# Tokens' low parts behind the next weight tile, list steps in a second queue, last transposes behind the product

## The chip, the cores and the metric

The kernel runs on one core of one Trainium2 chip. The metric is the device time of one execution in microseconds. Before the change the median of three runs is 1836.94 us (1836.01 to 1843.89). The engines are TensorE (PE), VectorE (DVE), ScalarE (ACT), GpSimd (POOL) and SyncE (SP, which here only issues DMAs).

## What is computed

Two blocks work on 512 tokens of width 1024 in float32. The first is an mLSTM and pooling mixer followed by a mixture of 32 experts; the second is a stick-breaking attention beside a gated spatial mixing. The change touches the experts alone. Cut to what matters:

```python
logits = xt @ w_router + b_router
top_vals, top_idx = lax.top_k(logits, 4)          # each token goes to 4 of 32 experts
top_gates = jax.nn.softmax(top_vals, axis=-1)
...
def expert_block(xb, e):                          # the rows of expert e
    gate = jnp.minimum(xb @ w_gate[e] + b_gate[e], 7.0)
    up = jnp.clip(xb @ w_up[e] + b_up[e], -7.0, 7.0)
    glu = gate * jax.nn.sigmoid(1.702 * gate)
    return (glu * (up + 1.0)) @ w_down[e] + b_down[e]
# each result times its gate, added to its token's row
```

Products are made in split precision: a float32 operand becomes a high part (a rounded cast) and a low part (the operand less its high part), and a product is the sum of high x high, high x low and low x high. What is split late or not at all is multiplied raw, at a slower rate.

## The kernel before

The experts are sorted by their number of tokens. A *wide* one has 112 rows (`C`), a *narrow* one 64 (`CS`); experts 0 and 1 and then every odd one to 29 are wide, the even ones from 2 to 28 and 30 and 31 are narrow. For a narrow one the high and low parts of the tokens lie side by side in one stationary operand (`xs`, `as`), so that two matmuls do what three do for a wide one.

`place(s)` is one step of the loop over experts: the gate product of expert s, the transposes of the previous expert's activated rows u into `aT`, the up product of s, the transposes of the next expert's tokens `xg` into `xT`, the gather of the tokens of s + 2, and the down product of s - 1 with its result and scatter. Each product (`product`, L921) goes through four weight tiles of 256 rows by 1024. SP loads the tiles (`wr`, 1 MB each) eight ahead, ACT makes the high part (`wh`, L145), DVE the low part (`wl`, L148), and `LEAD` = 3 tiles are split ahead of the product that uses them. The last tile of the products that have a raw part is not split: it is multiplied with `raws` at full float32.

Inside `manual_schedule` the order of the code is the order on each engine. The list `todo` holds small steps; `product` takes one after each weight tile. Among them are the activation of a narrow gate (`sg`), the clip and the product of u, and `lists`: at experts 1, 4, 8, 12, 16, 20 and 24 it puts four `marks` (L800, DVE) and one `rest` (L806 and following: 16 small matmuls `pl` and six small DVE operations) into `todo`. They make the row lists of four experts.

`parts_T` transposes and splits. A wide operand takes two PSUM tiles, of four transposes each: the first holds 4 of 8 blocks (128x448 when written as 112 columns each), the second 2 blocks that are split (128x224) and 2 raw ones. A narrow one takes one. `hilo` (L183) writes the high part on ACT and then the low part on DVE, which reads the PSUM tile as well as the high part. All of `tp`, `pl`, `pg` and the like come from `bank` (L108), which has two buffers:

```python
return self.ps.tile(list(shape), F32, name=name, tag="B", bufs=2)
```

The products' sums come from another pool (three buffers of two banks). After expert 8 stands a loop for lists that are longer than their expert's rows (`longer_lists`); with these inputs it makes no round. `gates_T`, `places` and `bias` prepare the last results; `before_last` and what follows it finish experts 30 and 31.

Of the kernel before, what the change touches and what calls it, by code (L numbers as in the profile page):

```python
# [25 lines left out]

WIDE = [True, True] + [False, True] * 14 + [False, False]
# [13 lines left out]
def f32(ap):  # L41
    return ap.bitcast(F32)
# [746 lines left out]
    return placed  # L789


def lists(k, places, entries, name, kinds, out, soon):


    nc, n, shp = k.nc, places.shape[2], [P, NTC, P]
    oh4 = k.b4("loh" if n == 1 else "oh4", (P, n, NTC, P), BF)

    def marks(e):
        slots = k.slots[:, kinds[e], None, :].to_broadcast(shp)
        nc.vector.tensor_tensor(oh4[:, e], slots, places[:, :, e, None].to_broadcast(shp), op=OP.is_equal)  # L800

    def rest():
        pt = k.bank("pl")
        for e in range(n):
            for c in range(NTC):
                nc.tensor.matmul(pt[:, 8 * e:8 * e + 5], oh4[:, e, c], entries[:, c, e], start=(c == 0), stop=(c == NTC - 1))  # L806
        L = pt[:, :8 * n].rearrange("p (e w) -> p e w", w=8)
        tok = k.small("tok" + name, [P, n], bufs=2)
        nc.vector.tensor_reduce(tok, L[:, :, :2], axis=X, op=OP.add)
        ti, tf, ga = (k.small(t + name, [P, n], dt, bufs=3) for t, dt in (("ti", I32), ("tf", F32), ("ga", F32)))  # L810
        for kind in sorted(set(kinds)):
            for odd in range(2):
                es = [e for e in range(odd, n, 2) if kinds[e] == kind]
                if es:
                    assert es == list(range(es[0], es[-1] + 1, 2))
                    es = slice(es[0], es[-1] + 1, 2)
                    rows_of(k, tok[:, es], ti[:, es], tf[:, es], kind)
        nc.vector.tensor_reduce(ga, L[:, :, 2:5], axis=X, op=OP.add)
        out.extend((ti[:, e:e + 1], ga[:, e:e + 1], tf[:, e:e + 1]) for e in range(n))

    for e in range(n):
        soon(lambda e=e: marks(e))
    soon(rest)


# [23 lines left out]
def moe(k):  # L849
    nc, tc, a = k.nc, k.tc, k.a  # L850
# [6 lines left out]

    info = []

    def listed(n, soon):  # L860

        s0 = max(2, listed.n)
        listed.n = s0 + n
        ss = slice(s0, s0 + n)
        lists(k, k.posm_s[:, :, ss], k.entry_s[:, :, ss], "l%d" % n, [int(not WIDE[s]) for s in range(s0, s0 + n)], info, soon)

    listed.n = 0
    ti, tf, placed = first_rows(k)
# [3 lines left out]
    k.depth = 9  # L872
    bias_g, bias_u = k.bias

    def raw_part(name, parity):

        return k.fixed["xr"][:, :2] if k.fixed else k.raws[:, 4 * "xa".index(name) + 2 * parity:][:, :2]

    def parts_T(src, name, parity, wide=True):


        if wide:
            hi, lo, raw = *(k.b4(name + n, (P, KD - 2, C), F32R) for n in "hl"), raw_part(name, parity)
            def use(k0, pt):
                n = min(4, KD - 2 - k0)
                k.ondve = k.hilo(pt[:, :n], hi[:, k0:k0 + n], lo[:, k0:k0 + n])
                if n < 4:
                    nc.scalar.copy(raw, pt[:, n:])  # L888

            k.transposes(src[:C], use)  # L890
            return hi, lo, raw
        x, pt = k.b4(name + "s", (P, KD, P), F32R), k.bank("tp", (P, KD, CS))
        for kk in range(KD):
            nc.tensor.transpose(pt[:, kk], src[:CS, kk * P:(kk + 1) * P], k.ident[:CS, :CS])  # L894
        if name == "x":
            k.hilo(pt, x[:, :, :CS], x[:, :, CS:])
            return x,
        k.hilo(pt[:, :KD - 2], x[:, :KD - 2, :CS], x[:, :KD - 2, CS:])
        raw = raw_part(name, parity)[:, :, :CS]
        nc.scalar.copy(raw, pt[:, KD - 2:])  # L900
        return x, raw

    def one_of(s):
        if s < 2:
# [7 lines left out]
    todo = []  # L912

    def product(xT, b, one, get):

        wide, raw = len(xT) == 3, xT[-1] if len(xT) > 1 else None
        p, n = k.bank2("pe"), C if wide else P
        for i in range(2 if b is not None else 0):
            nc.tensor.matmul(p[:n, i], one, b[:, i * 512:(i + 1) * 512], start=True, stop=False, skip_group_check=True)  # L919
        last = KD - 3 if raw is not None else KD - 1  # L920
        for k0 in range(0, KD, 2):  # L921
            w = get()
            for i in range(2):
                kk = k0 + i
                if len(w) == 1:
                    lr = (raw[:, i], w[0]),
                elif wide:
                    lr = (xT[0][:, kk], w[0]), (xT[0][:, kk], w[1]), (xT[1][:, kk], w[0])
                else:
                    lr = (xT[0][:, kk], w[0]), (xT[0][:, kk], w[1])  # L930
                for n_, (l, r) in enumerate(lr):
                    for j in range(2):
                        o = i * D + j * 512
                        nc.tensor.matmul(p[:l.shape[1], j], l, r[:, o:o + 512], start=(b is None and kk == 0 and n_ == 0),  # L934
                                         stop=(kk in (last, KD - 1) and n_ == len(lr) - 1), skip_group_check=True)
            if todo and not k.fixed:
                todo.pop(0)()
        return p[:n].rearrange("p a b -> p (a b)")

    lim = 7.0 / (1.0 + math.exp(-1.702 * 7.0))  # L940

    def soon(f):

        f() if k.fixed else todo.append(f)

    def added(p, name):

# [28 lines left out]
    def down(aT, get):  # L976
        return product(aT, None, None, get)
# [84 lines left out]
    listed(2, lambda f: f())  # L1062
    gather(xgs[0], info[2][0], C if WIDE[2] else CS)

    def place(s, u, xT, one):

        if s == 1 or s % 4 == 0 and s + 4 < NE:
            listed(4, todo.append)
        sg = gate(xT, one, k.next_w)
        aT = parts_T(u, "a", (s - 1) % 2, WIDE[s - 1])  # L1070
        u = up(sg, xT, one, k.next_w)
        if s + 1 < NE:
            one = one_of(s + 1)
            xT = parts_T(xgs[(s + 1) % 2], "x", (s + 1) % 2, WIDE[s + 1])
        if s < NE - 2:
            gather(xgs[s % 2], info[s + 2][0], C if WIDE[s + 2] else CS)
        if s < NE - 1:
            result(down(aT, k.next_w), *info[s - 1][:2])
        if s == NE - 3:
            todo.extend((lambda: places(k, [info[e][2] for e in (NE - 2, NE - 1)]), lambda: gates_T(k),  # L1080
                         lambda: bias(k, "b_down", 0.0, 3)))
        return u, xT, aT, one

    k.lead, k.depth, one = LEAD, DM, one_of(1)
    with tc.manual_schedule(engines=ALL_ENGINES):
        for s in range(1, LOOP_AT + 1):
            u, xT, aT, one = place(s, u, xT, one)
        while todo:
            todo.pop(0)()
    longer_lists()  # L1090
    with tc.manual_schedule(engines=ALL_ENGINES):
        for s in range(LOOP_AT + 1, NE):
            if s == NE - 2:
                k.stop = k.experts_end
            u, xT, aT, one = place(s, u, xT, one)
        aT1 = []
        todo.append(lambda: aT1.append(parts_T(u, "a", (NE - 1) % 2, WIDE[NE - 1])))
        k.depth = DE
        p = down(aT, k.next_w)
    k.lead = 0  # L1100
    with tc.manual_schedule(engines=IN_ORDER):
        before_last(k)
        k.depth = DE2
        k.ready += [k.parts() for _ in range(4 - len(k.ready))]
        ys = [weighted(p, info[NE - 2][1])]
        p = down(aT1[0], k.next_w)
# [34 lines left out]
        nc.vector.tensor_scalar(k.ohs[:, n], iof, tf, None, op0=OP.is_equal)  # L1141


def gates_T(k):

    nc, pg, g3 = k.nc, k.bank("pg3"), k.b4("g3", (P, NTC, 96))
    k.gT3 = k.b4("gT3", (96, S), F32R)
    nc.vector.tensor_copy(g3.rearrange("p c (r e) -> p c r e", r=3),
                          k.pg[:, :, 1, None, :].to_broadcast([P, NTC, 3, NE]))
# [331 lines left out]
```

## Time and profile before

| | |
|---|---|
| median of 3 runs | 1836.94 us |
| profiled execution | 1837.83 us |
| its span | 1836.1 us |
| PE busy | 1700.0 us (93%) |
| DVE busy | 1279.7 us (70%) |
| ACT busy | 1018.4 us (55%) |
| moved by DMA | 489.17 MB |

A profile row names an engine, a line and an operation as out<-in with the program's names. In the timeline the first number is the start in us, the second how long it lasted to the modelled end of the last one in it, `x2` how many it holds, and a bracket the idle time in front of it with what ended it. Matmuls overlap, so the start of the next one tells their pace. PEclk is the clock granted to PE, as a share of 2.4 GHz. Times are taken from one execution; the medians come from others.

### The profile page before, as it was taken

Reading aid. Unit: us, or ns where it says so; the run is one execution under the profiler, and the core shown is the slowest. Engines: PE = TensorE matmul, PEld = TensorE weight load, DVE = VectorE, ACT = ScalarE, POOL = GpSimd, SP = SyncE. Lnnn points to the kernel's source line nnn. Section 1 sums busy time; section 2 is a strip of 40 time slices with the busy share of each in tenths; the row PEclk is TensorE's granted clock in tenths of the full one; section 3 lists DMA queues with packets and bytes.
Section 4 is the critical chain, followed back from the end, with each engine's and each line's share of the span. In section 5 each row is a group of like instructions: output and inputs, shape, how many; then the busy total and the mean of one; then the engine's idle time right before and its main releaser. Section 6 shows DMA issues by size and latency. Waiting matters only on the chain.

```text
span 1836.1 us, 20169 instructions
## 1 busy us (share of the span) xinstructions
PE 1700.0 (93%) x7333; PEld 1222.6 (67%) x7333; DVE 1279.7 (70%) x1214; ACT 1018.4 (55%) x940; POOL 236.0 (13%) x211
## 2 busy tenths in 40 slices
PE   7989969989987999998998998999888999999997
PEld 5867846666664666666666666666566777777775
DVE  4766567787785887887887878878786247545352
ACT  4435345666664766765766666766674346542231
POOL 2012113101111011011011011011001100022001
PEclk9999989999998999999999999999988999999999
DMA  7225569999997999999999999999975301123241
GB/s 252 80 70 170 202 233 330 374 369 371 381 382 277 365 366 384 372 373 379 372 377 373 373 384 361 376 386 378 368 284 217 115 1 46 46 69 115 69 172 46
DMA packets 142328, 489.17 MB, mean 266 GB/s; under 512 B 10436, under 2 KB 11492, under 8 KB 142224
## 3 DMA queue, kind: packets, MB, share of 16 engines
q1 hardware_dynamic: 132176, 459.83, 66.3%
q0 software_dynamic: 8320, 21.72, 4.6%
q10 hardware_dynamic: 1728, 6.29, 0.9%
q8 instruction: 59, 0.97, 0.2%
q14 instruction: 45, 0.37, 0.1%
HBM read 474.52 MB, written 19.40 MB: 269 GB/s over the span
## 4 chain that ended last, share of the span: by engine, by line
PE 59%; DVE 5%; ACT 2%; issue 1%; POOL 1%; DMA 0%; another core or an unknown queue 0%; DVEq 0%; POOLq 0%; ACTq 0%
PE pe L934 36%; PE mm L189 5%; PE mm L190 5%; PE mm L191 5%; DVE wl L148 2%; PE pe L919 1%; PE z L1274 1%; ACT wh L145 1%; PE tp L213 1%; PE pa L1297 1%; PE tp L894 1%; PE ps L189 1%; PE ps L190 1%; PE ps L191 1%; DVE sg L950 1%
## 5 line engine op out<-in xcount | busy, mean ns | idle before, releaser
L148 DVE TENSOR_TENSOR wl<-wr,wh 128x2048 fp32r<-128x2048 f32 x365 | 826.1, 2287 | 271.1 <-ACT wh L145 230.7
L145 ACT CAST wh<-wr 128x2048 fp32r<-128x2048 f32 x365 | 681.2, 1900 | 154.3 <-PE pe L934 108.6
L934 PE MATMUL pe<-wr,raws 128*112 128x512 f32 (+1 forms) x512 | 232.6, 597 | 0.0
L934 PE MATMUL pe<-wl,xs 128*128 128x512 f32 x512 | 168.3, 411 | 15.9 <-DVE wl L148 15.9
L934 PE MATMUL pe<-wh,xs 128*128 128x512 f32 x512 | 169.1, 412 | 13.1 <-ACT wh L145 13.1
L988 POOL DMA_INDIRECT x1d<-y,til x28 | 73.8, 2634 | 830.5 <-ACT y L983 396.0
L934 PEld LDWEIGHTS pe<-wr,raws 128*112 128x112 f32 (+1 forms) x512 | 84.3, 167 | 112.9 <-issue 107.5
L934 PE MATMUL pe<-wh,xh 128*112 128x512 f32 x384 | 122.4, 400 | 10.0 <-issue 10.0
L934 PEld LDWEIGHTS pe<-wl,xs 128*128 128x128 f32 x512 | 99.9, 197 | 43.3 <-DVE wl L148 20.3
L934 PEld LDWEIGHTS pe<-wh,xs 128*128 128x128 f32 x512 | 100.2, 199 | 39.9 <-ACT wh L145 17.5
L934 PE MATMUL pe<-wl,xh 128*112 128x512 f32 x384 | 121.4, 398 | 0.0
L934 PE MATMUL pe<-wh,xl 128*112 128x512 f32 x384 | 121.0, 396 | 0.0
L190 PE MATMUL mm<-hTh,wl 128*128 128x512 f32 x296 | 117.1, 395 | 0.0
L191 PE MATMUL mm<-hTl,wh 128*128 128x512 f32 x296 | 116.8, 396 | 0.0
L189 PE MATMUL mm<-hTh,wh 128*128 128x512 f32 x296 | 115.7, 398 | 0.0
L189 PE MATMUL mm<-wh,hTh 128*128 128x512 f32 x256 | 104.0, 410 | 2.3 <-ACT v L1211 1.5
L190 PE MATMUL mm<-wh,hTl 128*128 128x512 f32 x256 | 102.5, 401 | 0.8 <-DVE hTl L185 0.8
L191 PE MATMUL mm<-wl,hTh 128*128 128x512 f32 x256 | 101.7, 399 | 0.0
L934 PEld LDWEIGHTS pe<-wh,xh 128*112 128x112 f32 x384 | 67.3, 177 | 32.7 <-issue 11.0
L934 PEld LDWEIGHTS pe<-wl,xh 128*112 128x112 f32 x384 | 67.6, 176 | 22.1
L934 PEld LDWEIGHTS pe<-wh,xl 128*112 128x112 f32 x384 | 67.5, 176 | 22.2
L888 ACT COPY raws<-tp 128x224 f32<-128x224 f32 x32 | 11.1, 346 | 118.2 <-DVE al L185 70.7
(435 smaller groups left out, 2514.0 us busy)
## 6 DMA issues: line engine op xcount, KB each, us to landing
wr<-in_w_gate SPq DMA_DIRECT2D x128, 1024.0 KB, 10.9
wr<-in_w_up SPq DMA_DIRECT2D x128, 1024.0 KB, 8.9
wr<-in_w_down SPq DMA_DIRECT2D x128, 1024.0 KB, 8.7
wr<-in_w_in SPq DMA_DIRECT2D x32, 1024.0 KB, 5.2
wr<-in_w_out SPq DMA_DIRECT2D x8, 1024.0 KB, 4.9
xt<-in_x SPq DMA_DIRECT2D x4, 512.0 KB, 10.5
x<-in_x POOLq DMA_DIRECT2D x4, 512.0 KB, 5.8
x1d<-x ACTq DMA_DIRECT2D x4, 512.0 KB, 2.8
```

What stands on the lines that cost most here:

```text
L145: self.nc.scalar.copy(hi[:, :n], t[:, :n])
L148: self.nc.vector.tensor_tensor(lo[:, :n], t[:, :n], f32(hi[:, :n]), op=OP.subtract)
L189: mm(ps, l[0], r[0], start=start, stop=False)
L190: mm(ps, l[1], r[0], start=False, stop=False)
L191: mm(ps, l[0], r[1], start=False, stop=stop)
L213: self.nc.tensor.transpose(pt[:, i], src[:, (k0 + i) * P:(k0 + i + 1) * P], self.ident[:n, :n])
L894: nc.tensor.transpose(pt[:, kk], src[:CS, kk * P:(kk + 1) * P], k.ident[:CS, :CS])
L919: nc.tensor.matmul(p[:n, i], one, b[:, i * 512:(i + 1) * 512], start=True, stop=False, skip_group_check=True)
L934: nc.tensor.matmul(p[:l.shape[1], j], l, r[:, o:o + 512], start=(b is None and kk == 0 and n_ == 0), stop=(kk in (last, KD - 1) and n_ == ...
L950: nc.vector.tensor_tensor(r, p[:CS], t, op=OP.add)
L988: nc.gpsimd.indirect_dma_start(out=k.x1d, out_offset=bass.IndirectOffsetOnAxis(ap=rows[:y.shape[0]], axis=0), in_=y, in_offset=None, bound ...
L1274: nc.tensor.matmul(zc[:, o:o + w], qT[rows, blk, c * P:w], kT[rows, blk, :w], start=(o == 0), stop=True, skip_group_check=True)
```

## The change

Five things are changed. `parts_T` no longer makes the low part behind the high part: on ACT the raw part is copied first, then the high part is made, and the low part on DVE becomes a step in `todo`, so it comes behind the next weight tile of the product that follows. Where `k.lead` is 0 (expert 0 and the last transposes) and in the loop it is made at once. Steps of `lists` go to a second list, `spare`, from which `product` takes only when `todo` is empty, and four empty steps stand between the marks and the rest. The steps `places`, `gates_T` and `bias` go to `spare` one expert earlier (at 28), `gates_T` is cut in two with three empty steps between. The last transposes, of expert 31's u, stand behind the whole down product of expert 30 instead of behind its third tile. The gate product of expert 0 is held until ACT's high part instead of DVE's low part.

```diff
 def lists(k, places, entries, name, kinds, out, soon, gap=0):
...
     for e in range(n):
         soon(lambda e=e: marks(e))
+    for _ in range(gap):
+        soon(None)
     soon(rest)
...
+    todo, spare = [], []
+
+    def soon(f):
+        todo.append(f) if k.lead and not k.fixed else f()
...
     def parts_T(src, name, parity, wide=True):
+        def low(out, src, hi):
+            soon(lambda: nc.vector.tensor_tensor(out, src, f32(hi), op=OP.subtract))
 
         if wide:
...
-                k.ondve = k.hilo(pt[:, :n], hi[:, k0:k0 + n], lo[:, k0:k0 + n])
                 if n < 4:
                     nc.scalar.copy(raw, pt[:, n:])
+                out = slice(k0, k0 + n)
+                k.onact4 = nc.scalar.copy(hi[:, out], pt[:, :n])
+                low(lo[:, out], pt[:, :n], hi[:, out])
...
-        k.hilo(pt[:, :KD - 2], x[:, :KD - 2, :CS], x[:, :KD - 2, CS:])
-        raw = raw_part(name, parity)[:, :, :CS]
-        nc.scalar.copy(raw, pt[:, KD - 2:])
+            raw, n = raw_part(name, parity)[:, :, :CS], KD - 2
+            nc.scalar.copy(raw, pt[:, n:])
+        nc.scalar.copy(x[:, :n, :CS], pt[:, :n])
+        low(x[:, :n, CS:], pt[:, :n], x[:, :n, :CS])
...
-            if todo and not k.fixed:
-                todo.pop(0)()
+            if (todo or spare) and not k.fixed:
+                ((todo or spare).pop(0) or int)()
...
-    def soon(f):
-        f() if k.fixed else todo.append(f)
...
-    with tc.issue_after(k.ondve.ins):
+    with tc.issue_after(k.onact4.ins):
         sg = gate(xT, one_of(0), k.next_w)
...
-            listed(4, todo.append)
+            listed(4, spare.append, 4)
...
-        if s == NE - 3:
-            todo.extend((lambda: places(k, [info[e][2] for e in (NE - 2, NE - 1)]), lambda: gates_T(k),
-                         lambda: bias(k, "b_down", 0.0, 3)))
+        if s == NE - 4:
+            spare.extend((lambda: places(k, [info[e][2] for e in (NE - 2, NE - 1)]), lambda: g3.append(gates_3(k)), None,
+                          None, None, lambda: gates_T(k, g3[0]), lambda: bias(k, "b_down", 0.0, 3)))
...
-        todo.append(lambda: aT1.append(parts_T(u, "a", (NE - 1) % 2, WIDE[NE - 1])))
         k.depth = DE
         p = down(aT, k.next_w)
-    k.lead = 0
+        k.lead = 0
+        assert not todo and not spare
+        aT1 = parts_T(u, "a", (NE - 1) % 2, WIDE[NE - 1])
```

In the rows of the program's order below, a number behind x says how many like instructions stand in a row. First DVE around the up product of expert 18, before the change; `wl` is the low part of a weight tile, `al` that of u of expert 17, `xl` that of the tokens of expert 19:

```order
L148 TENSOR_TENSOR wl<-wr,wh 128x2048 x4
L950 TENSOR_TENSOR sg<-pe,part 64x1024
L185 TENSOR_TENSOR al<-tp,ah 128x448
L185 TENSOR_TENSOR al<-tp,ah 128x224
L148 TENSOR_TENSOR wl<-wr,wh 128x2048 x4
L950 TENSOR_TENSOR u<-pe,part 64x1024
L185 TENSOR_TENSOR xl<-tp,xh 128x448
L185 TENSOR_TENSOR xl<-tp,xh 128x224
```

The same place on DVE with the change:

```order
L148 TENSOR_TENSOR wl<-wr,wh 128x2048 x4
L957 TENSOR_TENSOR sg<-pe,part 64x1024
L148 TENSOR_TENSOR wl<-wr,wh 128x2048 x2
L891 TENSOR_TENSOR al<-tp,ah 128x448
L148 TENSOR_TENSOR wl<-wr,wh 128x2048
L891 TENSOR_TENSOR al<-tp,ah 128x224
L148 TENSOR_TENSOR wl<-wr,wh 128x2048
L957 TENSOR_TENSOR u<-pe,part 64x1024
```

The two `al` moved behind two and three weight tiles' low parts, those of the last up tile and of the first two down tiles. On PE at the end of that up product, before the change, with the queues or engines that an instruction is made to wait for:

```order
L934 MATMUL pe<-wh,xs 128x512 x2
L934 MATMUL pe<-wl,xs 128x512 x2
L213 MATMUL tp<-ident,xg_1432 128x112 [waits DMASW6_49,PE_49]
L213 MATMUL tp<-ident,xg_1432 128x112 x3
L213 MATMUL tp<-ident,xg_1432 128x112 [waits PE_49]
L213 MATMUL tp<-ident,xg_1432 128x112 x3
L934 MATMUL pe<-wh,ah 112x512 [waits Activation_49]
```

And with the change:

```order
L945 MATMUL pe<-wh,xs 128x512 x2
L945 MATMUL pe<-wl,xs 128x512 x2
L213 MATMUL tp<-ident,xg_1432 128x112 [waits DMASW6_49,DVE_49,PE_49]
L213 MATMUL tp<-ident,xg_1432 128x112 x3
L213 MATMUL tp<-ident,xg_1432 128x112 [waits DVE_49,PE_49]
L213 MATMUL tp<-ident,xg_1432 128x112 x3
L945 MATMUL pe<-wh,ah 112x512 [waits Activation_49]
```

The transposes of the next tokens stand where they stood, but both groups of four now wait for DVE as well: for the last reader of the PSUM buffer that they write into. At the end of the experts, DVE before the change, from u of expert 31 on (`as` is the low part of that u, `yl` a result's):

```order
L950 TENSOR_TENSOR u<-pe,part 64x1024
L966 TENSOR_SCALAR u<-u 64x1024
L148 TENSOR_TENSOR wl<-wr,wh 128x2048
L973 SCALAR_TENSOR_TENSOR u<-sg,u 64x1024
L148 TENSOR_TENSOR wl<-wr,wh 128x2048
L185 TENSOR_TENSOR as<-tp,as 128x6x64
```

And with the change:

```order
L957 TENSOR_TENSOR u<-pe,part 64x1024
L973 TENSOR_SCALAR u<-u 64x1024
L148 TENSOR_TENSOR wl<-wr,wh 128x2048
L980 SCALAR_TENSOR_TENSOR u<-sg,u 64x1024
L148 TENSOR_TENSOR wl<-wr,wh 128x2048 x2
L891 TENSOR_TENSOR as<-tp,as 128x6x64
```

One more weight tile's low part now stands ahead of the last `as`.

## Rows read from the trace of the kernel before

**Rows 1.** The page: busy us, share, instructions; GB/s in forty equal slices.

```profile
PE 1700.0 (93%) x7333; PEld 1222.6 (67%) x7333; DVE 1279.7 (70%) x1214; ACT 1018.4 (55%) x940; POOL 236.0 (13%) x211
...
GB/s 252 80 70 170 202 233 330 374 369 371 381 382 277 365 366 384 372 373 379 372 377 373 373 384 361 376 386 378 368 284 217 115 1 46 46 69 115 69 172 46
```

**Rows 2.** Waits of PE: us in total, times, longest us.

```profile
PE pl L806 <- DVE al L185: 29.8, 6, 5.0
PE pe L934 <- DVE wl L148: 15.9, 10, 1.6
PE pe L934 <- ACT wh L145: 13.1, 10, 1.5
...
PE pe L934 <- issue: 10.0, 1, 10.0
...
PE pg L1151 <- DVE g L1148: 4.8, 1, 4.8
```

**Rows 3.** Timeline of PE, expert 18: start, us, operation, idle before.

```profile
904.40 0.74 PE L934 MATMUL pe<-wh,xs 128*128 128x512 f32 x2 [1.31 <-ACT wh L145]
906.73 0.73 PE L934 MATMUL pe<-wl,xs 128*128 128x512 f32 x2 [1.59 <-DVE wl L148]
907.29 0.62 PE L934 MATMUL pe<-wh,xs 128*128 128x512 f32 x2
...
908.22 0.93 PE L213 MATMUL tp<-ident,xg 112*128 112x112 f32 x8
908.92 0.70 PE L934 MATMUL pe<-wh,ah 128*112 128x512 f32 x2
```

**Rows 4.** Timeline of DVE at the same place.

```profile
900.13 1.21 DVE L950 TENSOR_TENSOR sg<-pe,part 64x1024 f32<-64x1024 f32 x1
...
904.38 2.29 DVE L148 TENSOR_TENSOR wl<-wr,wh 128x2048 fp32r<-128x2048 f32 x1 [2.21 <-ACT wh L145]
```

**Rows 5.** Timeline of ACT at the same place.

```profile
902.20 0.34 ACT L888 COPY raws<-tp 128x224 f32<-128x224 f32 x1 [3.78 <-DVE al L185]
902.44 1.90 ACT L145 CAST wh<-wr 128x2048 fp32r<-128x2048 f32 x1
904.24 1.06 ACT L955 ACTIVATE sg<-sg 64x1024 f32<-64x1024 f32 x1
905.21 5.50 ACT L145 CAST wh<-wr 128x2048 fp32r<-128x2048 f32 x3
```

**Rows 6.** Timeline of PE, expert 20, whose list steps run in it.

```profile
972.45 0.57 PE L806 MATMUL pl<-entry_s,oh 128*128 128x5 bf16 x16 [4.95 <-DVE al L185]
...
980.91 0.69 PE L934 MATMUL pe<-wh,ah 128*112 128x512 f32 x2
```

**Rows 7.** Timeline of DVE, expert 20.

```profile
970.66 1.21 DVE L950 TENSOR_TENSOR sg<-pe,part 64x1024 f32<-64x1024 f32 x1
...
974.90 2.29 DVE L148 TENSOR_TENSOR wl<-wr,wh 128x2048 fp32r<-128x2048 f32 x1 [2.21 <-ACT wh L145]
```

**Rows 8.** Windows: us, busy of five engines, PEclk, DMA share, GB/s.

```profile
1311.00:1317.60 6.60, 4.09 (x12) 3.37 (x13) 3.69 (x4) 2.38 (x2) 0.00 (x0) 0.50 1.04 327
904.00:910.00 6.00, 4.01 (x20) 2.88 (x21) 5.17 (x3) 6.00 (x5) 0.00 (x0) 1.00 1.03 414
969.50:976.50 7.00, 4.05 (x25) 3.27 (x25) 4.79 (x6) 3.77 (x3) 0.00 (x0) 0.52 1.03 413
1331.50:1338.30 6.80, 6.80 (x22) 4.72 (x21) 6.80 (x4) 4.66 (x5) 0.00 (x0) 0.50 0.81 314
1365.65:1369.00 3.35, 3.32 (x8) 2.65 (x9) 2.93 (x2) 3.35 (x3) 0.00 (x0) 0.50 0.31 128
```

**Rows 9.** Groups by form on DVE: count, busy us, mean ns.

```profile
L185 DVE TENSOR_TENSOR al<-tp,ah 128x448 fp32r<-128x448 f32 x16 | 9.7, 606 | 1.4 <-ACT ah L184 1.4
L185 DVE TENSOR_TENSOR al<-tp,ah 128x224 fp32r<-128x224 f32 x16 | 5.9, 371 | 0.0
```

**Rows 10.** Timeline of PE, raw tile of expert 30's down product.

```profile
1378.65 5.34 PE L934 MATMUL pe<-wr,raws 128*64 128x512 f32 x8
```

More of the change, by code (lines that the diff above doesn't have):

```diff
@@ L789, in rows_of, with lists @@
     return placed
-def lists(k, places, entries, name, kinds, out, soon):
+def lists(k, places, entries, name, kinds, out, soon, gap=0):
     nc, n, shp = k.nc, places.shape[2], [P, NTC, P]
@@ L858, in moe, with listed @@
     info = []
-    def listed(n, soon):
+    def listed(n, soon, gap=0):
         s0 = max(2, listed.n)
@@ L864, in listed @@
         ss = slice(s0, s0 + n)
-        lists(k, k.posm_s[:, :, ss], k.entry_s[:, :, ss], "l%d" % n, [int(not WIDE[s]) for s in range(s0, s0 + n)], info, soon)
+        lists(k, k.posm_s[:, :, ss], k.entry_s[:, :, ss], "l%d" % n, [int(not WIDE[s]) for s in range(s0, s0 + n)], info, soon, gap)
     listed.n = 0
@@ L894, in parts_T @@
             nc.tensor.transpose(pt[:, kk], src[:CS, kk * P:(kk + 1) * P], k.ident[:CS, :CS])
-        if name == "x":
-            k.hilo(pt, x[:, :, :CS], x[:, :, CS:])
-            return x,
-        k.hilo(pt[:, :KD - 2], x[:, :KD - 2, :CS], x[:, :KD - 2, CS:])
-        raw = raw_part(name, parity)[:, :, :CS]
-        nc.scalar.copy(raw, pt[:, KD - 2:])
-        return x, raw
+        raw, n = None, KD
+        if name == "a":
+            raw, n = raw_part(name, parity)[:, :, :CS], KD - 2
+            nc.scalar.copy(raw, pt[:, n:])
+        nc.scalar.copy(x[:, :n, :CS], pt[:, :n])
+        low(x[:, :n, CS:], pt[:, :n], x[:, :n, :CS])
+        return (x,) if raw is None else (x, raw)
     def one_of(s):
@@ L910, in one_of @@
         return one.rearrange("p a c -> p (a c)")
-    todo = []
     def product(xT, b, one, get):
@@ L1063, in moe @@
     gather(xgs[0], info[2][0], C if WIDE[2] else CS)
+    g3 = []
     def place(s, u, xT, one):
         if s == 1 or s % 4 == 0 and s + 4 < NE:
-            listed(4, todo.append)
+            listed(4, spare.append, 4)
         sg = gate(xT, one, k.next_w)
@@ L1087, in moe @@
             u, xT, aT, one = place(s, u, xT, one)
-        while todo:
-            todo.pop(0)()
+        for f in todo + spare:
+            (f or int)()
+        todo.clear()
+        spare.clear()
     longer_lists()
@@ L1095, in moe @@
             u, xT, aT, one = place(s, u, xT, one)
-        aT1 = []
-        todo.append(lambda: aT1.append(parts_T(u, "a", (NE - 1) % 2, WIDE[NE - 1])))
         k.depth = DE
         p = down(aT, k.next_w)
-    k.lead = 0
+        k.lead = 0
+        assert not todo and not spare
+        aT1 = parts_T(u, "a", (NE - 1) % 2, WIDE[NE - 1])
     with tc.manual_schedule(engines=IN_ORDER):
@@ L1105, in moe @@
         ys = [weighted(p, info[NE - 2][1])]
-        p = down(aT1[0], k.next_w)
+        p = down(aT1, k.next_w)
         k.wv = [k.next_w()]
@@ L1141, in places, with gates_3, gates_T @@
         nc.vector.tensor_scalar(k.ohs[:, n], iof, tf, None, op0=OP.is_equal)
-def gates_T(k):
-    nc, pg, g3 = k.nc, k.bank("pg3"), k.b4("g3", (P, NTC, 96))
+def gates_3(k):
+    g3 = k.b4("g3", (P, NTC, 96))
+    k.nc.vector.tensor_copy(g3.rearrange("p c (r e) -> p c r e", r=3),
+                            k.pg[:, :, 1, None, :].to_broadcast([P, NTC, 3, NE]))
+    return g3
+def gates_T(k, g3):
+    nc, pg = k.nc, k.bank("pg3")
     k.gT3 = k.b4("gT3", (96, S), F32R)
-    nc.vector.tensor_copy(g3.rearrange("p c (r e) -> p c r e", r=3),
-                          k.pg[:, :, 1, None, :].to_broadcast([P, NTC, 3, NE]))
     for c in range(NTC):
```

## The prediction

> **What bounds the kernel now.** I read the engines' shares first, then the waits of TensorE (PE), then the timeline around the places those waits come from, the granted clock there, and last what one operation costs. The profiled execution took 1837.83 us; its span is 1836.1. PE is busy 93% of it, and in the expert stretch the loads run at 361 to 386 GB/s in most slices [rows 1]. So PE sets the end, and only its gaps and its clock can give something back. The waits show where those gaps are [rows 2]: 29.8 us in six places where the list product of a narrow expert waits for VectorE's (DVE's) low part `al`; 13.1 + 15.9 us in ten places where a product waits for a weight tile's high and low part; 10.0 us at the loop; 4.8 us at the gate transposes near the end.
>
> There are two patterns. Call *A* a narrow expert without list steps (eight, besides the last two experts), and *B* one with them (six). In A, at expert 18, the last tile of the up product stops PE for 1.31 us and again for 1.59, and the down product begins at 908.92 [rows 3]. Going back: the tile's low part starts at 904.38 after 2.21 us of idle for its high part [rows 4]; ScalarE (ACT) had made that high part only from 902.44, because a copy of the raw part ahead of it waited 3.78 us for `al` [rows 5], and `al` stands behind `sg` on DVE. In B, at expert 20, four marks lengthen DVE's queue, PE stops 4.95 us and the down product begins at 980.91 [rows 6, 7]. The clock tells the two apart: it stays 1.00 around A's stop, and is 0.52 (mostly the 1.2 GHz level) from 969.5 to 976.5 in B [rows 8].
>
> **The change at A.** Removed: the raw copy no longer waits for `al`, so the high part of the last up tile is made while DVE is still busy, and `al` no longer stands ahead of that tile's low part. `sg` ends at 900.13 + 1.21 = 901.34; the low part takes 2.29 us, so PE can go on at 903.55, not 906.73: 3.2 us earlier. The up product ends at 908.22 - 3.18 = 905.04.
>
> Added: PE now waits for the deferred lows. All transposes take their PSUM from one pool of two buffers. The eight transposes of the next expert's tokens need both, and both hold u's transposes until the two `al` subtractions have read them. Before, these ran ahead of the last up tile. Now, DVE's order puts the first behind the low part of the first down tile, and the second behind one more. In times: ACT's activation of `sg` can start at 901.34 and holds ACT some 0.96 us (its 1.06 less the overlap to the next start, 904.24 to 905.21 before), the high part of the first down tile takes 1.90 and ends at 904.2 [rows 5]; its low part, at a spacing of 2.20, lasts to 906.43; the first `al`, 0.606 [rows 9], to 907.03. PE has then been idle from 905.04 to 907.07. Four transposes (0.4 us; eight took 0.70) follow; the next low part lasts to 909.2, the second `al` (0.37) to 909.53, and PE has been idle another 2.1 us. After four more transposes the down product begins at 909.95, against 908.92: **+1.0 us**. Behind the waiting transposes stands the whole of PE's queue; ahead of them nothing is left.
>
> The clock is the dispute. Idle of 2.9 us in two pieces left it at 1.00 at expert 18; 4.95 us brought it to half [rows 6, 8]. The same two pieces at experts 30 and 31 (the last two of the ten stops, 1.6 and at most 1.5 us) were followed by 6.8 and 3.35 us at 0.50 [rows 2, 8]. The new gap has 4.1 us of idle with 0.4 us of transposes inside. I take a half-clock stretch of 3.4 us behind it, the shorter of those two, which costs half of that: **1.7**; the ends are 0 and 3.4. So A costs 2.7 (1.0 to 4.4), times eight: **+21.6**.
>
> The Trainium skill, "TensorE: Matmul & The Clock Gate", section "A second HAM failure mode: psum-queue depth-cycling", speaks against this change: where a kernel cycles through PSUM banks and PE idles briefly between groups of matmuls, the clock swings between its levels and the matmuls in between lose throughput. By that rule every A loses its clock, and the sum is the one I take; by expert 18's own stop, which kept its clock, it would be 8 us for the eight. Experts 30 and 31 agree with the rule, expert 18 does not.
>
> **At B.** The marks stay where they were; the list product and its six small DVE steps move to the next expert's gate, so the 4.95 us stop goes, and with it 1.8 us that the half clock took when PE resumed. In its place: `sg` ends at 970.66 + 1.21 = 971.87, so the last up tile's low part starts there, not at 974.90, and ends at 974.1 [rows 7]; the two tiles that stood behind the list product take PE 3.7 us (16 pairs at 0.47) from 967.5, where its 4.95 us of idle began, so it has run dry by then and waits some 2.4 us. The up product ends at 975.55, then come the two bank waits as in A (2.07 and 2.1), and the down product begins at 980.5 instead of 980.91: -0.4. The list product's 0.5 us [rows 6] is paid later, in the next gate: +0.5. The clock falls again, as it did: +1.9. Together **+2.0** each (0.2 with no clock lost, 3.7 with twice as much), times six: **+12**.
>
> **At the loop.** Eight more matmuls of gate 9 stand ahead of the loop's branch; they run in PE's 10.0 us of idle there [rows 2]: **-1.5**, at some 0.2 us each (four took 0.93 from 907.29 to 908.22 [rows 3]). What releases PE, the scatter of expert 7, is the same.
>
> **At the end.** The gate transposes' copy now comes an expert earlier and three empty steps ahead of them: the 4.81 us go, and half of the 4.1 us that PE then ran at 0.50, 2.0 [rows 2, 8]. At expert 30 the up product's stop (2.9) and its half clock (3.4 of 6.8) go; in their place comes one bank wait of 2.1, for one bank only, since expert 31 is narrow, and 0.6 us of the moved steps in expert 29; I put 1.0 of lost clock beside them: 4.8 + 2.0 + 2.9 + 3.4 - 3.7 = 9.4. At expert 31 the stop (1.6 and about 1) and half of 3.35 us go, 4.3; but the product of expert 30 now waits some 2 us for its deferred `as`, and may lose 1. The last transposes move behind the raw tile, which before took 5.34 us at half clock in front of the last product [rows 10]. That tile now runs while `u` is made; but the last `as` stands behind two weight low parts on DVE (before behind one): 2.2 us later than it might be, so what the tile gives back is lost to this wait, within 1 us. Say -1.5. Both: **-11** (-8 to -15).
>
> All other moved steps (the wide experts' lows, the lows of the next tokens) I cost at nothing: their consumers start at least one tile later, and DVE is busy 70% of the span [rows 1]; if that cover is gone, 0.3 to 0.6 us of `al` or `xl` [rows 9] appear per expert, at most 10 us. No DMA is added; gate 0 is released by a high part rather than a low one, 0.4 us at most.
>
> Sum: 21.6 + 12 - 1.5 - 11 = +21 on the profiled 1837.8, which is 1859; the median of the runs is 0.9 below the profiled one: **1858 us**.
>
> **Rivals.**
> *R1, the waits are exchanged and the clock holds.* For it: expert 18 kept 1.00 through 2.9 us. Against: 4.1 us is nearer to B's 4.95. Eight times 1.0, six times 0.2, -1.5, and -12.5 at the end where little clock is lost: about -5, **1832 us**, which counts as no change.
> *R2, the waits vanish: faster.* DVE idles 2.21 us in A and in B at the very place [rows 4, 7]; if the low parts ran far enough ahead that both `al` came before the up product's end, A would give 2.9, B 4.95 + 1.8 - 0.5 and the end 12: some 70 us. It needs DVE 4 us ahead of what its order and durations give, and loads at about 400 GB/s over the whole stretch, where short pieces show 414 [rows 8] but most slices 361 to 386. So I take half: **1800 us**. It decides when `al` ends before 905.0 in A.
> *R3, the clock stays low longer,* as the 6.8 us behind expert 30's stop show: another 1.7 us at fourteen places, +24, **1882 us**.
> *R4, the faster side by the end alone:* if neither A nor B moves, the end and the loop give -12.5, 1824 us. I put it with R2.
>
> **Chances.** My forecast 0.55 (its own range 1846 to 1874), R1 0.22, R2 with R4 0.13, R3 0.10. A change of 0.5% (9.2 us) is about what can be told from none, so "the same" is 1827.8 to 1846.1. R1 lies in it nearly whole; 0.02 of R1 and R2 go over the bound either way, and 0.02 of my own case falls below 1846: faster 0.14, same 0.23, slower 0.63. The range reaches down to R1 with its spread and up to R3: 1828 to 1880.
>
> **What would show it.** In the changed profile, PE's waits should no longer hold a list product waiting for `al`, nor most waits for weight parts in narrow experts; instead token transposes should wait for `al`, twice in each of fourteen narrow experts, about 2 us each, some 55 us in all, and the clock should be at half for 3 to 4 us of the down product behind them. The 4.8 us wait of the gate transposes should be gone. It would prove me wrong if the transposes wait less than 1 us each, or if they wait 2 us and the clock stays at 1.00 (R1), or if PE now waits for a weight DMA.

## The result and the profile after

The changed kernel takes 1859.61 us (median of 20 runs, 1857.74 to 1864.15), the kernel before 1839.89 in the runs beside it: a ratio of 1.0098, 95% interval [1.0077, 1.0118]. It is about 1% slower. The kernel before scatters more (1835.28 to 1861.59 us), and its longer runs have the lower clock: in those beside the first experiment, 1838.54 us at a mean granted clock of 0.969 and 1862.88 at 0.955. The profiled execution of the changed kernel has a span of 1857.9 us, 21.8 more than the profiled one before.

The page of the changed kernel, the two rows that answer to [rows 1]:

```profile
PE 1717.7 (92%) x7333; PEld 1233.3 (66%) x7333; DVE 1282.2 (69%) x1214; ACT 1015.9 (55%) x940; POOL 222.8 (12%) x211
...
GB/s 249 80 69 188 200 236 320 377 362 346 383 364 279 374 352 358 367 359 369 358 377 354 347 374 370 334 388 373 354 353 236 125 1 46 46 68 114 68 170 45
```

PE is busy 17.7 us longer with the same 7333 matmuls: they ran slower, so part of the loss is clock, not waiting. The loads run slower than before in most slices, but they are not what holds PE: ScalarE's waits list none for a weight of an expert.

PE's waits in the changed kernel (columns as in [rows 2]):

```profile
PE tp L213 <- DVE al L891: 28.7, 15, 2.0
PE tp L213 <- issue: 24.5, 13, 1.9
PE pe L945 <- DVE wl L148: 14.1, 14, 1.8
...
PE pe L945 <- issue: 5.6, 1, 5.6
PE pe L945 <- DVE as L891: 4.7, 2, 2.8
```

The list product's 29.8 us, the 13.1 for `wh` and the gate transposes' 4.8 are gone. The 14.1 us for `wl` are almost all B's (0.4 and 1.8 us at expert 20, where 2.4 were forecast). In place of the others, token transposes wait 28 times for about 1.9 us, 53.2 us in all. Of half of these the view says "issue", but the timelines below show what ended them: DVE's first `al` ends at 923.83, and the transposes start at 923.93.

Timeline of PE in expert 18, the place of [rows 3]; everything there lies 16.7 us later than before (the up product's bias starts at 913.56, not 896.82):

```profile
921.36 0.63 PE L945 MATMUL pe<-wl,xs 128*128 128x512 f32 x2
923.93 0.57 PE L213 MATMUL tp<-ident,xg 112*128 112x112 f32 x4 [1.94 <-issue]
926.47 0.70 PE L213 MATMUL tp<-ident,xg 112*128 112x112 f32 x4 [1.97 <-DVE al L891]
926.85 1.18 PE L945 MATMUL pe<-wh,ah 128*112 128x512 f32 x2
927.82 1.05 PE L945 MATMUL pe<-wl,ah 128*112 128x512 f32 x2
```

And DVE there, the place of [rows 4]:

```profile
916.87 1.21 DVE L957 TENSOR_TENSOR sg<-pe,part 64x1024 f32<-64x1024 f32 x1
918.00 2.27 DVE L148 TENSOR_TENSOR wl<-wr,wh 128x2048 fp32r<-128x2048 f32 x1
921.00 2.29 DVE L148 TENSOR_TENSOR wl<-wr,wh 128x2048 fp32r<-128x2048 f32 x1 [0.72 <-ACT wh L145]
923.21 0.62 DVE L891 TENSOR_TENSOR al<-tp,ah 128x448 fp32r<-128x448 f32 x1
923.74 2.28 DVE L148 TENSOR_TENSOR wl<-wr,wh 128x2048 fp32r<-128x2048 f32 x1
925.94 0.38 DVE L891 TENSOR_TENSOR al<-tp,ah 128x224 fp32r<-128x224 f32 x1
```

Each group of four transposes starts about 0.1 us after the `al` that frees its PSUM buffer, and each `al` stands behind a weight tile's low part of 2.3 us. The stop that was there before is gone: the last up tile's low part runs from 918.00, right behind `sg`.

The clock around it (columns as in [rows 8]):

```profile
914.00:921.90 7.90, 7.85 (x34) 5.82 (x32) 7.18 (x5) 6.97 (x8) 0.00 (x0) 1.00 1.03 380
921.90:926.80 4.90, 0.99 (x9) 0.75 (x9) 4.90 (x5) 4.20 (x4) 0.00 (x0) 1.00 1.02 409
926.80:930.30 3.50, 3.50 (x11) 2.59 (x10) 3.46 (x4) 2.39 (x3) 0.00 (x0) 0.51 1.03 412
930.30:936.80 6.50, 6.50 (x29) 4.88 (x28) 6.24 (x5) 2.17 (x2) 0.00 (x0) 1.00 1.03 409
```

For 4.9 us PE is busy 0.99; then it works for 3.5 us at half clock, before it is back at 1.00.

Where the 21.8 us of span come from, by the starts of the bias matmuls that open each gate and up product in the two traces:

| place | forecast, us | measured, us |
|---|---|---|
| A, eight experts | +21.6 | +24.0 (2.6 to 3.5 each) |
| B, six, with the list product in the next gate | +12 | +13.0 |
| loop | -1.5 | -4.6 |
| expert 30, with the moved steps in 29 | -9.4 | -9.5 |
| expert 31 and the end | -1.5 | -1.4 |
| all else | 0 | +0.3 |

### The profile page after: what moved, and what is told of

Read it like the earlier page. It is cut to its first block, busy times and chain, and to the rows that moved or that the text cites. A ratio compares the mean times of both kernels' runs of the same rounds, so it can differ in the third digit from the quotient of the medians.

```text
span 1857.9 us, 20174 instructions
## 1 busy us (share of the span) xinstructions
PE 1717.7 (92%) x7333; PEld 1233.3 (66%) x7333; DVE 1282.2 (69%) x1214; ACT 1015.9 (55%) x940; POOL 222.8 (12%) x211
## 4 chain that ended last, share of the span: by engine, by line
PE 57%; DVE 4%; issue 3%; ACT 2%; DMA 1%; POOL 0%; another core or an unknown queue 0%; DVEq 0%; SPq 0%; POOLq 0%; ACTq 0%
PE pe L945 35%; PE mm L189 5%; PE mm L190 5%; PE mm L191 5%; DVE wl L148 2%; PE pe L930 1%; ACT wh L145 1%; PE tp L213 1%; PE z L1291 1%; PE pa L1314 1%; PE tp L907 1%; PE ps L189 1%; PE ps L190 1%; PE ps L191 1%; DVE sg L957 1%
## 5 line engine op out<-in xcount | busy, mean ns | idle before, releaser
L945 PE MATMUL pe<-wl,xs 128*128 128x512 f32 x512 | 162.8, 399 | 14.7 <-DVE wl L148 14.1
L945 PE MATMUL pe<-wh,xs 128*128 128x512 f32 x512 | 160.1, 394 | 0.0
L995 POOL DMA_INDIRECT x1d<-y,til x28 | 49.4, 1764 | 855.8 <-DVE y L994 409.1
L945 PEld LDWEIGHTS pe<-wl,xs 128*128 128x128 f32 x512 | 94.6, 188 | 44.6 <-DVE wl L148 24.3
L945 PEld LDWEIGHTS pe<-wh,xs 128*128 128x128 f32 x512 | 96.1, 188 | 22.2
L856 POOL DMA_INDIRECT xg<-h2d,til x30 | 78.2, 2605 | 70.4 <-DVE tfl L788 39.6
L213 PE MATMUL tp<-ident,xg 112*128 112x112 f32 x128 | 24.6, 334 | 64.8 <-DVE al L891 28.7
```

Source lines behind the costliest of these rows:

```text
L213: self.nc.tensor.transpose(pt[:, i], src[:, (k0 + i) * P:(k0 + i + 1) * P], self.ident[:n, :n])
L856: nc.gpsimd.indirect_dma_start(out=xg[:n], out_offset=None, in_=k.h2d, in_offset=bass.IndirectOffsetOnAxis(ap=rows[:n], axis=0), bounds_ch ...
L995: nc.gpsimd.indirect_dma_start(out=k.x1d, out_offset=bass.IndirectOffsetOnAxis(ap=rows[:y.shape[0]], axis=0), in_=y, in_offset=None, bound ...
```

## The experiments

Theory T is the prediction's: the low parts that come late hold both PSUM buffers, the token transposes wait for them, and the clock falls behind that wait; the other parts of the change are gains. The rivals are named in each expectation. All times of places below are up and down product together, from bias matmul to bias matmul, against the trace of before. The diffs are cut to what matters.

**The parts one by one.** First the changed kernel with the low parts made at once:

```diff
         def low(out, src, hi):
-            soon(lambda: nc.vector.tensor_tensor(out, src, f32(hi), op=OP.subtract))
+            nc.vector.tensor_tensor(out, src, f32(hi), op=OP.subtract)
```

> The changed kernel, but every low part is made right behind its high part instead of as a step behind the next weight tile; raw copy first, second queue, gap and end as changed. Theory T (the loss is the two PSUM waits of the token transposes in each narrow expert, plus the half clock behind them): both waits go, the last up tile's low part starts behind sg and two al (about 902.2 instead of 904.4 in A), so A is 2.3 us shorter than before the change, eight times -18; B loses the 4.95 us stop for one of about 3.3 and pays 0.5 for the list product: -1.5 to -3.3, six times -15; loop -4.6 and end -11 as in the changed kernel. In all some -49 against before: 1790 us (1775 to 1805). Rival Q (the second queue, the gap or the end cost the time): stays above 1850. Rival L (the loads bound the expert stretch, so PE's time cannot be won): 1830 to 1840.

Measured: 1793.84 us, ratio to before 0.9738 [0.9689, 0.9788]. The deferral alone separates a kernel 1% slower from one 2.6% faster. A is 2.3 to 2.4 us shorter than before in all eight, B 1.3 to 3.0. PE's waits in it:

```profile
PE pe L945 <- DVE wl L148: 27.6, 23, 2.6
...
PE pe L945 <- issue: 11.6, 1, 11.6
```

No transposes of u or of expert tokens wait for a low part any more; what is left is the last up tile's low part, the loop, and 4.2 us for the last `as`. Theory T holds, rivals Q and L fall.

Next, the kernel before with the raw copy first:

```diff
                 n = min(4, KD - 2 - k0)
-                k.ondve = k.hilo(pt[:, :n], hi[:, k0:k0 + n], lo[:, k0:k0 + n])
                 if n < 4:
                     nc.scalar.copy(raw, pt[:, n:])
+                k.ondve = k.hilo(pt[:, :n], hi[:, k0:k0 + n], lo[:, k0:k0 + n])
...
-        k.hilo(pt[:, :KD - 2], x[:, :KD - 2, :CS], x[:, :KD - 2, CS:])
         raw = raw_part(name, parity)[:, :, :CS]
         nc.scalar.copy(raw, pt[:, KD - 2:])
+        k.hilo(pt[:, :KD - 2], x[:, :KD - 2, :CS], x[:, :KD - 2, CS:])
```

> The kernel before with one thing of the change: on ACT the raw part is copied ahead of the high part, so it no longer waits for the low part. Theory T: in A the last up tile's high part no longer waits, the stop of 2.9 us shrinks to some 0.7, ten places -2.2 each, and at experts 30 and 31 the half clock goes too (-5); B keeps its stop at the list product. In all -22 to -28: 1812 us (1805 to 1820). Rival L (loads bound the stretch): within 5 us of before. Rival Q says nothing on it.

Measured: 1810.09 us, 0.9819 [0.9772, 0.9865]. A is 2.3 to 2.5 us shorter in all eight, expert 30 5.6; B moved by -0.4 to +0.9 and kept its stop (29.8 us for `al` at the list product, as in [rows 2]). Swapping two copies on ACT gives the larger part of what the first experiment won.

The kernel before with the list steps in the second queue, four empty steps behind the marks, all else as before:

```diff
-            if todo and not k.fixed:
-                todo.pop(0)()
+            if (todo or spare) and not k.fixed:
+                ((todo or spare).pop(0) or int)()
...
-            listed(4, todo.append)
+            listed(4, spare.append, 4)
```

> The kernel before with the list steps in the second queue and four empty steps behind the marks; lows at once, raw copy behind them, end as before. Theory T: B's 4.95 us stop becomes an A-like stop of 3 to 5 us with the half clock moved behind it, and 0.5 us of list product moves on: near 0 each; the loop's idle may shrink by up to 4.6. 1834 us (1828 to 1842). Rival Q (the second queue costs the time): 1850 or more.

Measured: 1848.42 us, 1.0031 [0.9994, 1.0068]: no difference that can be told, and 6 us above the expected range. The stop at the list product is gone, but its waits moved to the last up tile:

```profile
PE pe L936 <- ACT wh L145: 32.1, 16, 3.1
PE pe L936 <- DVE wl L148: 25.4, 22, 1.6
```

B became 0.6 to 2.1 us longer, where I expected nothing. The half clock now falls behind the stop as a whole (at expert 20, 4.9 us of matmuls at half pace, against some 4 before), which is a likely cause, not a shown one. The loop did not gain. In the profiled execution five A, which this edit does not touch, were longer too, by 1.3 to 2.8 us, at a clock of 0.72 to 0.86 where it had been 1.00; the last section comes back to this.

The kernel before with its end alone changed:

```diff
-        if s == NE - 3:
-            todo.extend((lambda: places(...), lambda: gates_T(k), lambda: bias(k, "b_down", 0.0, 3)))
+        if s == NE - 4:
+            todo.extend((lambda: places(...), lambda: g3.append(gates_3(k)), int,
+                         int, int, lambda: gates_T(k, g3[0]), lambda: bias(k, "b_down", 0.0, 3)))
...
-        todo.append(lambda: aT1.append(parts_T(u, "a", (NE - 1) % 2, WIDE[NE - 1])))
         k.depth = DE
         p = down(aT, k.next_w)
+        aT1 = [parts_T(u, "a", (NE - 1) % 2, WIDE[NE - 1])]
```

> The kernel before with the end alone changed: places, gates (in two steps with three empty ones between) and bias from the end of expert 28 on, last transposes behind the whole down product of expert 30. Theory T: the 4.8 us stop at the gate transposes and 2 us of its half clock go, 0.6 is added, the last transposes give -1 to +2. -5 to -7: 1833 us (1828 to 1838). Rival Q (the end costs time): 1842 or more.

Measured: 1831.86 us, 0.9925 [0.9890, 0.9959]; the gate of expert 30 is 7.4 us shorter. The time is as expected.

**The clock by itself.** The changed kernel with its waits left in place, and PE given work during them:

```diff
+    def fill():
+        if len(filler) == 1:
+            filler.append(k.bank2("dm"))
+        x0, pd = filler
+        for i in range(9):
+            nc.tensor.matmul(pd[:, i % 2], x0[:, 0], x0[:, 0:4], start=True, stop=True, skip_group_check=True)
...
         for k0 in range(0, src.shape[1] // P, 4):
+            if fill:
+                fill()
             pt = self.bank("tp", (P, 4, P))[:, :, :n]
```

> The changed kernel with nine extra matmuls of 128x512 (some 2.1 us at full clock) ahead of each of the two groups of token transposes in a narrow expert, on operands that are there, into a PSUM tile of the products' pool that nobody reads: PE is given work for the time that it waits for the two deferred low parts; both waits themselves stay. Theory T (of the 2.6 to 3.5 us that an A lost, 1.0 to 1.2 is the later start and the rest the half clock behind it): the down product starts within 0.3 us of where it does in the changed kernel, and the clock stays at 1.00 behind it, so A is +1.0 to +1.5 against before, B near +0.3: 25 us less than the changed kernel, 1836 us (1828 to 1845). Rival C (the half clock costs nothing, something else slows the down product): 1857 to 1866.

Measured: 1835.78 us, 0.9962 [0.9934, 0.9990] of before. PE at expert 18 in it:

```profile
907.80 2.24 PE L897 MATMUL dm<-xs 128*128 128x512 f32 x9
909.90 0.57 PE L215 MATMUL tp<-ident,xg 112*128 112x112 f32 x4
910.24 2.31 PE L897 MATMUL dm<-xs 128*128 128x512 f32 x9
912.44 0.57 PE L215 MATMUL tp<-ident,xg 112*128 112x112 f32 x4
912.79 0.69 PE L957 MATMUL pe<-wh,ah 128*112 128x512 f32 x2
```

And its clock there:

```profile
907.80:912.70 4.90, 4.90 (x26) 3.75 (x25) 4.90 (x5) 4.29 (x4) 0.00 (x0) 1.00 1.02 408
912.70:916.20 3.50, 3.50 (x19) 2.70 (x18) 3.46 (x3) 2.77 (x4) 0.00 (x0) 1.00 1.03 412
```

From the last matmuls of the up product (907.34) to the first of the down product it is 5.45 us, and 5.49 in the changed kernel: the waits are there still. But the 3.5 us behind them hold 19 matmuls instead of 11, and the clock is 1.00 behind the waits in all eight A (0.50 to 0.69 in the changed kernel). A is 1.0 to 1.4 us longer than before, in place of 2.6 to 3.5. So of A's mean +3.0, 1.1 is the later start and 1.9 the half clock; eighteen useless matmuls win the 1.9 back. Rival C falls, and this is the prediction's R1 made by hand: had the clock held, the change would have come out within half a percent of before.

**The wait by itself.** The changed kernel with the low parts one weight tile earlier, in a queue ahead of the others:

```diff
-            soon(lambda: nc.vector.tensor_tensor(out, src, f32(hi), op=OP.subtract))
+            f = lambda: nc.vector.tensor_tensor(out, src, f32(hi), op=OP.subtract)
+            first.append(f) if k.lead and not k.fixed else f()
...
-                ((todo or spare).pop(0) or int)()
+                ((first or todo or spare).pop(0) or int)()
```

> The changed kernel with the low parts in a queue of their own that is taken before the other steps, so that the two al come one weight tile earlier (behind the last up tile's low part and behind the first down tile's) and the activation of sg two tiles later. Theory T: in A the first transposes wait no more, the second some 1.3 us; down begins 1.8 us earlier than before the change, the clock holds: 8 times -1.8; B -2 each; loop and end as in the changed kernel: -42, 1797 us (1785 to 1812). Rival (it is not the PSUM wait but the deferral as such, any one): 1845 or more.

Measured: 1813.00 us, 0.9850 [0.9803, 0.9897], 1 us above the range that I expected. Its profiled execution has a span of 1803.9. A is 1.7 to 2.0 us shorter, as expected, with the clock at 1.00 behind the wait in all eight, and B 0.9 to 3.3; the loop took 1.6 us more than before where I put -4.6, and the gate of expert 31 took 4.8 more, which I did not foresee. The waits of the transposes:

```profile
PE tp L213 <- DVE al L891: 13.2, 13, 1.1
```

In A, one wait of 1.0 us instead of two of 1.9: deferral as such does no harm, only its length.

I also tried to take the wait away by giving the transposes' pool four buffers, and the products' two instead of three:

```diff
-        return self.ps.tile(list(shape), F32, name=name, tag="A", bufs=3)
+        return self.ps.tile(list(shape), F32, name=name, tag="A", bufs=2)
...
-        return self.ps.tile(list(shape), F32, name=name, tag="B", bufs=2)
+        return self.ps.tile(list(shape), F32, name=name, tag="B", bufs=4)
```

> The changed kernel with four buffers instead of two in the pool of the transposes and two instead of three (of two banks each) in that of the products. Theory T: the token transposes find a free buffer and wait for no low part; in A down begins at about 905.7 on the time scale of before instead of 908.9 (-3.2, eight times -25), in B some -4.2 (six times -25), loop -4.6, end -11: -66, 1773 us, if a product never waits for one of the two remaining buffers. Rival L (the loads bound the stretch at some 400 GB/s): 1785 to 1800, with waits of ACT for weights. Rival (two product buffers are too few): above 1800, with products waiting for the adds.

> The kernel before with the same two pools changed (four and two buffers): what the pools alone do. Theory T: nothing in the experts, since no transposes wait there: within 5 us of before. Were the two product buffers too few, it would be slower by the same as in the changed kernel with them.

Measured: 2048.29 us with the change (1.1118 [1.1065, 1.1171]) and 2051.42 without (1.1135 [1.1075, 1.1195]). This is the third case, two product buffers are too few; PE's waits in the changed kernel with these pools:

```profile
PE pe L930 <- DVE sg L957: 58.9, 16, 4.9
PE pe L945 <- DVE u L957: 58.2, 16, 4.3
PE pe L930 <- DVE y L994: 35.2, 14, 2.5
```

The token transposes' waits for `al` are indeed absent, and the change then costs nothing against the same pools without it. That shows what the waits are for, the two buffers, since the low parts are still deferred. But the price drowns any gain, and on the time the experiment says nothing.

**A version that beats both.** If B's loss in the first experiment was its four marks on DVE, the list steps belong into a wide expert. This is the first experiment's kernel, with them begun there:

```diff
-        if s == 1 or s % 4 == 0 and s + 4 < NE:
-            listed(4, spare.append, 4)
+        if s % 4 == 1 and s + 4 < NE:
+            listed(4, spare.append, 3)
```

> The changed kernel with lows at once (as e1) and the list steps begun in wide experts (1, 5, 9, ... 25) instead of 1 and the narrow 4, 8, ... 24; three empty steps behind the marks. Theory T: what B still lost in e1 against A (four marks of 0.6 us ahead of the last up tile's low part, and half clock behind the stop) goes: up and down together 21.3 us as in A instead of 24.4 to 27.0, six times some -4; the marks are hidden in a wide expert's gate. 24 less than e1: 1770 us (1764 to 1780). Rival L (the loads bound the expert stretch near 400 GB/s): 1782 to 1794, with waits of ACT for weights.

Measured: 1787.83 us, 0.9679 [0.9643, 0.9716]. B went to 21.2 us (23.1 at expert 8, ahead of the loop), the same as A, 6.1 to 6.3 shorter than before, as expected. The time did not follow: 6 us less than the first experiment's median (11 by the two ratios), not 24. In the profiled execution B's gain over the first experiment is 24.9 us, and most of it goes again: 3.9 in the wide experts that now hold the list steps, 3.6 at the loop, some 9 from expert 28 on, and 4.5 in the attention of the second block, which no edit touches (last section). The loop now held PE for 15.5 us, and ACT waits for the experts' weights, 58 us in all (1.5 us in the first experiment):

```profile
ACT wh L145 <- DMA wr<-in_w_down: 27.2, 22, 3.6
ACT wh L145 <- DMA wr<-in_w_gate: 17.6, 20, 2.5
...
ACT wh L145 <- DMA wr<-in_w_up: 13.5, 14, 2.7
```

Last, the same kernel with both low parts of a tile as one step behind the first weight tile, in a queue `first` as above:

```diff
-            if (first or todo or spare) and not k.fixed:
-                ((first or todo or spare).pop(0) or int)()
+            while first and not k.fixed:
+                first.pop(0)()
+            if (todo or spare) and not k.fixed:
+                ((todo or spare).pop(0) or int)()
```

> As e9, but both low parts of a tile come together as one step behind the next product's first weight tile, ahead of the other steps: behind one weight tile's low part (the last up tile's) and ahead of that of the first down tile. Theory T: on the time scale of before, the last up tile's low part ends at 903.55 (up product ends 905.04) and both al by 904.5, before the token transposes need the buffers; down begins at about 905.8 instead of 906.6 in e9: fourteen times -0.9 and no stop over 1 us: 1758 us (1750 to 1768). Rival L: no faster than e9.

Measured: 1786.35 us, 0.9666 [0.9628, 0.9704]. Narrow experts fell to 20.8 us (22.6 at expert 8) up to expert 20 (0.4 less than in the run above, not 0.9), and then went up to 22.0 to 22.5. ACT's waits for weights grew:

```profile
ACT wh L145 <- DMA wr<-in_w_down: 41.3, 33, 4.9
ACT wh L145 <- DMA wr<-in_w_gate: 25.6, 28, 2.5
ACT wh L145 <- DMA wr<-in_w_up: 25.5, 24, 2.2
```

Rival L, which fell in the first experiment, holds here for the later experts: ACT begins to wait for their weights some 800 us into the span in this run, some 1000 us in the one above. It is not the whole of what is missing: this run too loses 4.5 us in the second block. From 600 to 1200 us into the span, the loads run like this (columns as in [rows 8]); before:

```profile
600.00:1200.00 600.00, 565.52 (x2364) 387.62 (x2363) 490.40 (x336) 401.78 (x304) 77.30 (x34) 0.98 0.99 374
```

With the low parts at once, in the first experiment:

```profile
600.00:1200.00 600.00, 583.16 (x2453) 400.48 (x2453) 502.96 (x346) 414.37 (x313) 58.41 (x36) 0.99 1.01 385
```

With the lists in wide experts and the lows grouped, in the last:

```profile
600.00:1200.00 600.00, 594.24 (x2513) 406.55 (x2513) 516.17 (x351) 425.66 (x319) 87.20 (x37) 1.00 1.02 392
```

The run with the lists in wide experts and lows at once has 392 GB/s as well. While ACT waited most, from 1000 to 1240 us, both moved 391 to 392 GB/s, no more than in the stretch before. So 392 is about where the loads set the pace; before, at 374, they were 5% away.

## Why the prediction was right, point by point

*The wait.* Expert 18 on the scale of before, forecast and measured (less 16.74): up product's end 905.04 and 905.25, first transposes 907.07 and 907.19, second 909.57 and 909.73, down product 909.95 and 910.11. The step held to 0.2 us, because it was worked out from DVE's order, not from the edit's distance in the code. That the wait is for the two PSUM buffers, the pool of four showed; that its length matters and not the deferral, the queue ahead of the others.

*The clock.* Taken at 1.7 per A between 0 and 3.4, it was 1.9 by the filler; the size was right, but it had been taken from other stops (experts 30 and 31), not worked out. Expert 18's own quiet stop was no guide for a longer one: all eight A lost their clock. The Trainium skill, "TensorE: Matmul & The Clock Gate", section "A second HAM failure mode: psum-queue depth-cycling", says of such cycling through PSUM banks, with PE idle for a moment between groups, that the clock swings and costs throughput. The trace agrees, with 0.51 for 3.5 us behind the bank waits of expert 18; behind the one shorter wait of the queue ahead of the others (at most 1.1 us), A kept 1.00.

*B.* +2.2 each, against +2.0, and by its parts: the down product begins no earlier (forecast -0.4), the list product took 0.3 to 0.4 in the five next gates (forecast 0.5), and the rest, 1.9, is the half clock (forecast 1.9). One slip in the working did no harm: the two tiles ahead of the stop are 8 pairs of matmuls, not 16; at 0.47 us a pair they take the 3.7 us that it used.

*The loop* is the term that was mis-sized: -4.6, not -1.5. The eight matmuls that moved in front of it take 1.8 us (the prediction's own row, four in 0.93, gives 1.9). The other part is the scatter that releases PE, which I took as it was. In the changed kernel, and then before (start, us, and what ended the idle time ahead of it; `loh` is set when the scatter has landed):

```profile
572.04 1.53 POOL L995 DMA_INDIRECT x1d<-y,til  x1 [0.89 <-ACTq L1016]
577.79 0.10 POOL L1013 MEMSET loh<- 128x1 bf16 x1 [4.05 <-DMA x1d<-y,til]
```

```profile
560.74 3.64 POOL L988 DMA_INDIRECT x1d<-y,til  x1 [2.02 <-SPq L1009]
569.04 0.10 POOL L1006 MEMSET loh<- 128x1 bf16 x1 [4.49 <-DMA x1d<-y,til]
```

PE goes on 3.6 us behind `loh` in both. The scatter landed 5.7 us after its issue, and 8.3 before: 2.6 us of the gain. In the experiments too the wait at the loop goes with it: 6.0 us where the scatter took 6.1, 12.3 where it took 10.5; only the last two kernels wait some 5 us longer than that. Why the landing takes 5.7 to 11.2 us is not shown.

*The end.* Both terms came within 0.1 us, of which some is luck. At expert 30 the gate gave 7.5 us instead of 6.8 and the up and down products 2.4 instead of 3.2, and the moved steps cost 0.4 instead of 0.6. The -1.5 for expert 31 and what follows was the rest of terms of 4.3, 2 and 1. That the last `as` is late shows in the waits as 2.8 us of 4.7 (two waits of products for `as`).

*The edits put at nothing.* Wide experts' up and down stayed within 0.06 us, but for 1 (-0.5) and 29 (+0.4, the moved steps, forecast 0.6).

*The rivals.* R1 needed the clock to hold through both waits; it did so only with the filler. R2 needed DVE 4 us further ahead; with the lows at once the same place gained 5.4 us per A against the change, so the gain was there, behind another order.

## What to carry to other kernels

A reader of a PSUM buffer that is put off puts off whoever writes that buffer next: before you defer a step, list what it releases, and read the wait from the order of the engine that does it. A stop of a few us on TensorE costs its own length and the half clock behind it; if the wait can't go, work that nobody needs can hold the clock. When PE's stops are taken away one after another, look at what the next engine or queue has left: here the loads were 5% away.

## What the runs showed of the hardware that was not expected

The clock's answer to a stop of the same length is not the same each time. In the experiment that changes only the end, whose A are those of before, PE at expert 2:

```profile
332.25 0.73 PE L934 MATMUL pe<-wh,xs 128*128 128x512 f32 x2 [1.39 <-ACT wh L145]
334.57 1.22 PE L934 MATMUL pe<-wl,xs 128*128 128x512 f32 x2 [1.59 <-DVE wl L148]
```

and at expert 14 of the same execution:

```profile
773.19 0.73 PE L934 MATMUL pe<-wh,xs 128*128 128x512 f32 x2 [1.32 <-ACT wh L145]
775.52 0.73 PE L934 MATMUL pe<-wl,xs 128*128 128x512 f32 x2 [1.59 <-DVE wl L148]
```

The pair of matmuls takes 1.22 us behind the first stop, at half clock, and 0.73 behind the second, and the places were 2.7 us longer and 0.0 longer than in the trace of before. Two stops of 0.07 us difference lie on both sides. So a stop of about 3 us in two pieces is not safe, even where one trace shows the clock holding behind it, as [rows 8] did at expert 18. In the changed kernel, with 3.9 us, all eight A lost it. Eighteen matmuls whose result is thrown away held it in all eight.

The clock also fell where PE had no stop at all. In the second block the same matmuls of the attention, which no edit touches, ran at half clock with the lists in wide experts (first row) and at full clock in the first experiment (second row), with PE busy throughout in both, and in the 45 us ahead of them:

```profile
1435.19:1440.00 4.81, 4.81 (x12) 2.23 (x12) 3.50 (x4) 3.83 (x4) 0.00 (x0) 0.50 0.00 2
1441.19:1443.90 2.71, 2.71 (x12) 1.34 (x12) 2.71 (x3) 2.71 (x3) 0.00 (x0) 1.00 0.00 0
```

It was at 0.50 to 0.52 there in three of the ten traces with the pools as before (the lists in the second queue, and the last two kernels), at 1.00 in seven, and it cost 4.5 us in the last two. What decides it no run shows.
